# A decoder kernel's opening: a third buffer for early weight pieces, a fixed order on VectorE, C earlier, x loaded by chunk

## The chip, the cores and the metric

The kernel runs on one core of a Trainium2 chip. The metric is the device time of one execution in microseconds (us); less is better. The core's engines work side by side, each through its own queue in order: TensorE (PE) for matmuls, VectorE (DVE), ScalarE (ACT), GpSimd (POOL), and SyncE (SP), which issues most of the DMAs. Times in the trace count from the span's start.

## The reference, cut to what matters

x is (1, 256, 2048) in float32. There are two layers, each a mixer and a SwiGLU feed-forward, with RMSNorm ahead of both.

```python
# layer 0: S5, a diagonal complex state space, 128 groups of 16 channels and 64 states
bu = einsum('blgc,gpc->blgp', norm(x), bb)            # complex
s[k] = lb * s[k-1] + bu[k]                            # scan over the 256 tokens
y = einsum(s_re, c_re) - einsum(s_im, c_im) + d_skip * norm(x)
g = gelu(y); gl = g @ w_glu                           # 2048 x 4096
h = x + gl[..., :2048] * sigmoid(gl[..., 2048:])
h = h + swiglu(norm(h))                               # 2048 -> 5632 -> 2048
# layer 1: sliding-window attention, 32 heads, then the same feed-forward, then a last RMSNorm
```

## The kernel before, in words

Everything is float32. A large matrix product takes each operand as two parts, high and low, and adds three products (`products`, L763). The weights come in 332 pieces of 512 x 512. Each piece is loaded by SP (L107, 1 MB, two raw buffers), then split: ACT copies the high half (L121), DVE subtracts it from the piece for the low half (L122). `Weights.place` says where the two halves go, a tile of 16 KB per partition: three places in rotation, two from the pool `wq` and one from `wp`. `wp` is opened only after the S5 stage has closed its pool, so pieces 0 to 5 have two places. `Weights.next` gives the next piece, and splits up to two further ones and loads up to four further ones ahead. For each piece PE does 24 matmuls (L765 to L767) against 512 columns.

The S5 stage (`s5`) works on 64 pairs of groups, in two halves of 32 pairs and four quarters `t`. Tokens are cut into 64 chunks of four, so that a state steps once per chunk. First x is normed into `xs` (`scaled`, L398, by half). `products(t)` makes the input tables X[t] with POOL (L419) and DVE (L424, L427), ACT copying one part. `tokens(t)` turns xs into U on PE (L436). `states(t, b)` turns X on PE (L448), multiplies with U (L459), and ACT copies the sums into V of the half (L461). Then `step(hf)` (L497, L500, L502) is one step of that half's scan on DVE, three operations; each half has 62 of them, each dependent on the last.

Beside that: `pc` and `dd` (L506, L508) turn the skip weights `d_skip` from `drows`, which POOL fills (L267). POOL makes Cq (L560 to L562), PE and ACT turn it into Cg and C1 (L571, L577). POOL makes the tables T from Cg (`first_states`). `kernels(hf)` makes the tables M on PE (L613 to L625) for the tokens of the same chunk (`own_tokens`, L647). `copied` (L656) brings the scan's states from V to St, and `outputs` (L669) multiplies St with T. `end(qs, ...)` does the outputs of two quarters `q`, GELU (L676), and turns the result into gt, high half on ACT (L690), low half on DVE (L691). (0, 2) are the quarters of the first half, (1, 3) of the second.

Four weight pieces of GLU's first chunk (`EARLY = 4`) are used inside S5, on gt of the first half, while the second scan still runs. Pieces 4 to 7 follow on gt of the second half (`glu`, c == 0), then the other chunks of GLU, with two accumulations `pa` and `pb` for 512 columns each. At the end of a chunk, h gets the product (L880 to L882). x is loaded into h, two DMAs of 1 MB (L1108). Steps put in `left` run between the pieces of a later product.

The order of instructions on each engine is not the program's. A planner simulates the engines: of the instructions that it takes as ready, it puts the one that stands first in the program. `pin` (`keep_in_program_order`) ties an instruction behind the one traced just before it on its engine, and does nothing else: instructions traced after a pinned one can still be put ahead of it. A tile of a tag has that tag's count of buffers, and a new tile waits for the release of an older one.

Of the kernel before, what the change touches and what calls it, by code (L numbers as in the profile page):

```python
# [9 lines left out]
F32 = mybir.dt.float32  # L10
# [7 lines left out]
P = 128  # L18
# [10 lines left out]
NS = 64  # L29
GC = 16  # L30
EARLY = 4
L = 4
NK = T // L
PAIRS = G // 2
# [12 lines left out]
def bc(ap, axis, n):  # L47

    v = ap.unsqueeze(axis)
    shape = list(v.shape)  # L50
    shape[axis] = n
    return v.to_broadcast(shape)
# [3 lines left out]
def kernel(  # L56
# [22 lines left out]
    def bank(shape, name="ps"):  # L79
        return ps.tile(shape, F32, tag="ps", name=nm(name))  # L80
# [9 lines left out]
    class Weights:  # L90
        def __init__(self):
            self.src, self.raw, self.hl = [], [], []
            self.early = {}
            self.used = 0
            self.limit = 0

# [12 lines left out]

        def place(self, i):  # L110

            pool, n = (wp, 1) if i % 3 == 0 and i > 3 else (wq, 2)
            return pool.tile([P, 2, 4, 512], F32R, tag="w", name=nm("w"), bufs=n)

        def split(self, upto, keep=lambda ins: ins):
# [69 lines left out]
    def s5(early_piece):  # L185
# [3 lines left out]
        with st:  # L189
# [3 lines left out]
            def big(shape, name):  # L193
                return sp.tile(shape, F32, tag="b8", name=nm(name), bufs=5)
# [5 lines left out]
                return slice(g2 * NS, (g2 + 1) * NS)  # L200


            Vt = [sp.tile([P, NK, 2, 32], F32, name=f"V{hf}") for hf in range(2)]

            U = sp.tile([P, 4, 16, NK], F32, name="U")

# [57 lines left out]

            drows = sp.tile([PAIRS, 2, L, GC], F32, name="drows")
            PL.memset(drows, 0.0)
            PL.tensor_copy(drows[:, :, 3], drow.rearrange("a (g c) -> a g c", g=2))  # L267


            gb = [bank([P, 512], "gb") for _ in range(2)]  # L270
# [145 lines left out]
            def products(t):  # L416
                tmp = big([P, 3, 2, 16, GC], "tmp")
                for j in (2, 1, 0):
                    PL.tensor_tensor(tmp[:, j], bc(LIs[:, 2 - j].rearrange("p (h f) -> p h f", h=2)  # L419
                                                   [:, :, 16 * t : 16 * t + 16], 3, GC),  # L420
                                     of_groups(B2, t), op=ALU.mult)
                for j in (2, 1, 0):
                    pa = bank([P, 2, 16, GC], "pa")
                    V.tensor_tensor(pa, bc(LR[:, 2 - j].rearrange("p (h f) -> p h f", h=2)  # L424
                                           [:, :, 16 * t : 16 * t + 16], 3, GC),
                                    of_groups(B1, t), op=ALU.mult)
                    V.tensor_tensor(X[t][:, :, :, j].rearrange("p a g c -> p (a g) c"),  # L427
                                    pa.rearrange("p h f c -> p (h f) c"),
                                    tmp[:, j].rearrange("p h f c -> p (h f) c"), op=ALU.add)
                S.copy(X[t][:, :, :, 3].rearrange("p (h a) g c -> p h (a g) c", h=2), of_groups(B1, t))  # L430

            def tokens(t):
                for b in range(2):
                    pu = bank([P, 4, 2, NK], "pu")
                    for i in range(4):
                        PE.transpose(  # L436
                            pu[:, i].rearrange("p h k -> p (h k)"),
                            xs[:, t // 2, 8 * (t % 2) + 4 * b + i].rearrange("p g j c -> p (g j c)"), ident,
                        )
                    S.copy(  # L440
                        U[:, t].rearrange("p (h a) k -> p h a k", h=2)[:, :, 4 * b : 4 * b + 4],
                        pu.rearrange("p a h k -> p h a k"),
                    )
# [21 lines left out]
            def states(t, b):  # L465
                ahead.append((t, b, turned_x(t, b)))
                if len(ahead) > 1:
                    flush()

            def flush():  # L470
                t, b, xt = ahead.pop(0)
                added(t, b, xt)
# [5 lines left out]
            def scan_tables(hf):  # L478
                scan.append(bank([P, 2, 2, 2, 32], "scan"))
                re, im = (LPT[:, 3, ri].rearrange("p (h f a) -> p f h a", h=2, f=2)[:, hf] for ri in range(2))  # L480
                for o, v, f in ((0, re, 1.0), (1, re, 1.0), (2, im, 1.0), (3, im, -1.0)):
                    S.mul(scan[hf][:, 0, o // 2, o % 2].rearrange("p (h a) -> p h a", h=2), v, f)
# [1 line left out]

            reached = [1, 1]

            def step(hf, parts=1):

                reached[hf] += 1
                k = reached[hf]  # L490
                n = 32 // parts
                ws, pr = scan[hf][:, 0], scan[hf][:, 1]
                vs = []
                for i in range(parts):
                    part = slice(n * i, n * (i + 1))
                    t_ = pr[..., part]
                    V.tensor_tensor(t_, ws[..., part], bc(Vt[hf][:, k - 1, :, part], 1, 2), op=ALU.mult)  # L497
                    vs.append((Vt[hf][:, k, :, part], t_))
                for v, t_ in vs:
                    V.tensor_tensor(v, v, t_[:, 0], op=ALU.add)  # L500
                for v, t_ in vs:
                    V.tensor_tensor(v, v, t_[:, 1, ::-1], op=ALU.add)  # L502


            pc = bank([P, PAIRS], "pc")
            PE.transpose(pc, drows.rearrange("a g j c -> a (g j c)"), ident[:PAIRS, :PAIRS])  # L506
            dd = lp.tile([P, PAIRS, GC], F32, name="dd")
            V.tensor_tensor(dd, bc(pc, 2, GC), bc(idm, 1, PAIRS), op=ALU.mult)  # L508
            products(0)
            tokens(0)  # L510
            products(1)
# [4 lines left out]
                states(0, b)  # L516
            scan_tables(0)
            products(2)
            products(3)
            for b in range(4):  # L520
                states(1, b)
# [15 lines left out]
            V.tensor_tensor(u, u, w, op=ALU.subtract)  # L537
            V.tensor_tensor(q_[:, 1], u, iv, op=ALU.mult)

            step(0)  # L540
            step(0)
            tokens(2)
            step(0)
            for b in range(4):
                states(2, b)
                step(0)
                step(0)
            tokens(3)
            scan_tables(1)
            for b in range(4):  # L550
                states(3, b)
                step(0)
                step(0)
            flush()


            Cq = big([G, GC, 2, NS], "Cq")
            c2 = big([G, GC, 2, NS], "c2")
# [7 lines left out]
            for ri in range(2):  # L566
                for e in range(2):
                    pt = bank([P, 8, PAIRS], "pc")
                    for c in range(8):
                        for g2 in range(2):  # L570
                            PE.matmul(pt[rows(g2), c], Cq[:, 8 * e + c, ri], ident[:, g2::2], start=True, stop=True)  # L571
                    S.mul(Cg[:, ri, :, 8 * e : 8 * e + 8], pt.rearrange("p c a -> p a c"), 1.0 - 2 * ri)
            C1 = big([P, G, GC], "C1")
            for i in range(GC // 4):
                pt = bank([P, 4, G], "pc")
# [141 lines left out]
            while reached[0] < NK - 1:  # L717
                step(0)
                if reached[0] + 1 in cuts:
                    k1 = reached[0] + 1  # L720
                    for q in (0, 2):
                        pin(copied(q, cuts[cuts.index(k1) - 1], k1))
                if reached[0] < NK - 1:
                    step(1)

            W.split(1, pin)
            for i in range(4):
                step(1)

            def early():  # L730
                early_piece(gt, 0, 0)
                for q in (1, 3):
                    St[q] = big([P, 2, 16, NK], "St")
                    pin(copied(q, 0, 32))
                for half, q in ((0, 2), (1, 0), (1, 2)):
                    early_piece(gt, half, q)

            end((0, 2), early, lambda: None, pin)
            while reached[1] < NK - 1:
                step(1)  # L740
            for q in (1, 3):
                own_tokens(q)
                pin(copied(q, 32, NK))
            end((1, 3), lambda: None, lambda: W.split(EARLY + 1, pin))
        return gt

    def rms_scale(pool, ssq, shape, keep=lambda ins: ins, between=lambda: None):
# [116 lines left out]
        return wp.tile([P, 512], F32, tag=name, name=nm(name), bufs=bufs)  # L864

    def glu(norm):
        for c in range(NCH):
            if c == 0:
                pa, pb = accs
                for _, half, q in G_ORDER[EARLY:8]:  # L870
                    piece(accs[half], gt[q], q == 0, q == 3)
                while left:
                    left.pop(0)()
            else:
                pa = linear(gt)
                pb = linear(gt)
            for t in range(2):
                hc = h[t][:, 512 * c : 512 * c + 512]
                sg = tmp2("act")
                S.activation(sg, pb[t], AF.Sigmoid)  # L880
                V.tensor_tensor(sg, pa[t], sg, op=ALU.mult)
                V.tensor_tensor(hc, hc, sg, op=ALU.add)  # L882
                norm.chunk(c, t)
# [219 lines left out]
    wp = ctx.enter_context(tc.tile_pool(name="wp", bufs=1))  # L1103
    h = [wp.tile([P, D], F32, name=f"h{t}") for t in range(2)]

    def load_h():
        for t in range(2):
            nc.sync.dma_start(h[t], x[t * P : (t + 1) * P, :])  # L1108

    left.append(load_h)  # L1110

    n0 = Norm(0)
    glu(n0)
    n1 = Norm(1)
# [32 lines left out]
```

## Time and profile before

| | |
|---|---|
| time, median of 3 runs | 2056.07 us (2054.76 to 2057.02) |
| time of the profiled execution | 2056.38 us |
| its span | 2054.6 us |
| PE busy | 1995.3 us (97%), 10692 matmuls |
| DVE busy | 1090.7 us (53%) |
| ACT busy | 859.1 us (42%) |
| POOL busy | 86.2 us (4%) |
| weights' high halves (L121), low halves (L122) | 332 of 1.916 us, 332 of 2.295 us |
| HBM read | 356.90 MB, 175 GB/s over the span |

The profiled execution's time is 1.8 us longer than its span. The page cuts the span into 40 slices of 51 us and gives each engine's busy share in tenths: PE has 6, 8, 7, 8 in the first four slices and 9 in nearly all the others. The line PEclk has 8, 9, 8, 9 there and 9 after (9 is 90% or more). So what isn't PE's own work lies almost wholly in the first 200 us, the S5 stage and GLU's beginning.

### The profile page before, as it was taken

The page shows a single profiled execution, that of the slowest core. Times are in us where ns is not written, and L with a number is a line of the kernel's source. Part 1 is how long each engine was busy: PE and PEld are TensorE (multiplying, and loading weights), DVE is VectorE, ACT ScalarE, POOL GpSimd, SP SyncE. Part 2 cuts the span into 40 slices and gives each one's busy share as a digit, 9 for nine tenths or more (in the row PEclk, how much of TensorE's full clock was granted, in tenths as well). Part 3 has the DMA queues.
Part 4 walks back from the last instruction along what each step waited for, and adds up shares of the span by engine and source line. Part 5 has one row for each costly group of instructions (what it writes and reads, how often), then busy time and mean ns, then how long its engine had stood idle before and what let it go on. Part 6 is the DMA issues. An engine that isn't in the chain of part 4 may idle for free.

```text
span 2054.6 us, 25198 instructions
## 1 busy us (share of the span) xinstructions
PE 1995.3 (97%) x10692; PEld 1648.8 (80%) x10692; DVE 1090.7 (53%) x1347; ACT 859.1 (42%) x867; POOL 86.2 (4%) x66
## 2 busy tenths in 40 slices
PE   6878999999999999999999999999999999999998
PEld 5766888888888888888887777888888888888886
DVE  6955445444544454454466775544454445444545
ACT  5544445334334433433455445443333343343333
POOL 5630000000000000000000000000000000000000
PEclk8989999999999999999999999999999999999999
DMA  5026566555556555555555434565566555555564
GB/s 126 2 83 216 185 187 197 190 186 192 195 186 191 190 192 191 190 193 186 183 186 173 130 102 160 174 196 187 185 195 194 186 194 194 186 192 195 184 194 154
DMA packets 182514, 360.62 MB, mean 176 GB/s; under 512 B 10369, under 2 KB 10433, under 8 KB 182017
## 3 DMA queue, kind: packets, MB, share of 16 engines
q1 hardware_dynamic: 181392, 355.56, 53.7%
q8 instruction: 83, 1.36, 0.3%
q10 hardware_dynamic: 578, 2.14, 0.3%
q0 software_dynamic: 432, 1.33, 0.2%
q14 instruction: 29, 0.24, 0.0%
HBM read 356.90 MB, written 2.10 MB: 175 GB/s over the span
## 4 chain that ended last, share of the span: by engine, by line
PE 92%; DVE 4%; ACT 1%; issue 1%; DMA 1%; POOL 0%; SPq 0%; DVEq 0%; ACTq 0%; POOLq 0%
PE acc L767 29%; PE acc L765 29%; PE acc L766 29%; DVE scan L497 1%; PE tr L894 1%; PE pv L459 1%; DVE w L122 1%; DVE V L502 1%; DVE V L500 1%; ACT w L121 1%; PE tr L805 1%; PE po L1041 0%; PE tr L1030 0%; POOL tmp L419 0%; PE px L448 0%
## 5 line engine op out<-in xcount | busy, mean ns | idle before, releaser
L122 DVE TENSOR_TENSOR w<-raw,w 128x2048 fp32r<-128x2048 f32 x332 | 761.8, 2295 | 856.2 <-ACT w L121 856.2
L121 ACT ACTIVATE w<-raw 128x2048 fp32r<-128x2048 f32 x332 | 636.0, 1916 | 968.4 <-PE acc L767 845.8
L765 PE MATMUL acc<-w,xT 128*128 128x512 f32 x1568 | 613.6, 391 | 0.0
L767 PE MATMUL acc<-w,xT 128*128 128x512 f32 x1568 | 612.1, 390 | 0.0
L766 PE MATMUL acc<-w,xT 128*128 128x512 f32 x1568 | 611.5, 390 | 0.0
L767 PEld LDWEIGHTS acc<-w,xT 128*128 128x128 f32 x1568 | 294.5, 188 | 61.9 <-issue 1.0
L765 PEld LDWEIGHTS acc<-w,xT 128*128 128x128 f32 x1568 | 294.6, 188 | 61.1 <-issue 1.3
L766 PEld LDWEIGHTS acc<-w,xT 128*128 128x128 f32 x1568 | 294.7, 188 | 60.5 <-issue 0.5
L765 PE MATMUL acc<-w,hT 128*128 128x512 f32 x704 | 275.6, 391 | 0.0
L766 PE MATMUL acc<-w,hT 128*128 128x512 f32 x704 | 273.9, 390 | 0.0
L767 PE MATMUL acc<-w,hT 128*128 128x512 f32 x704 | 273.8, 390 | 0.0
L765 PEld LDWEIGHTS acc<-w,hT 128*128 128x128 f32 x704 | 132.3, 188 | 27.9 <-ACT hT L896 1.2
L767 PEld LDWEIGHTS acc<-w,hT 128*128 128x128 f32 x704 | 132.2, 188 | 27.6
L766 PEld LDWEIGHTS acc<-w,hT 128*128 128x128 f32 x704 | 132.3, 188 | 27.0
L767 PE MATMUL acc<-w,gt 128*128 128x512 f32 x256 | 102.2, 400 | 4.4 <-DVE gt L691 4.4
L765 PE MATMUL acc<-w,gt 128*128 128x512 f32 x256 | 102.2, 399 | 3.7 <-ACT w L121 3.7
L766 PE MATMUL acc<-w,gt 128*128 128x512 f32 x256 | 102.1, 399 | 1.9 <-DVE w L122 1.9
L767 PEld LDWEIGHTS acc<-w,gt 128*128 128x128 f32 x256 | 49.4, 193 | 15.7 <-DVE gt L691 5.3
L765 PEld LDWEIGHTS acc<-w,gt 128*128 128x128 f32 x256 | 49.4, 193 | 14.5 <-ACT w L121 4.1
L766 PEld LDWEIGHTS acc<-w,gt 128*128 128x128 f32 x256 | 49.5, 193 | 12.3 <-DVE w L122 2.2
L921 DVE TENSOR_TENSOR h<-h,acc 128x512 f32<-128x512 f32 x64 | 43.5, 687 | 24.7 <-PE acc L767 24.7
L907 ACT ACTIVATE act<-acc,ry 128x512 f32<-128x512 f32 x44 | 30.2, 690 | 59.8 <-PE acc L767 59.8
(240 smaller groups left out, 1225.0 us busy)
## 6 DMA issues: line engine op xcount, KB each, us to landing
raw<-in_ffn_w_gate_dram SPq DMA_DIRECT2D x88, 1024.0 KB, 5.2
raw<-in_ffn_w_up_dram SPq DMA_DIRECT2D x88, 1024.0 KB, 5.2
raw<-in_ffn_w_down_dram SPq DMA_DIRECT2D x88, 1024.0 KB, 5.1
raw<-in_s_w_glu_dram SPq DMA_DIRECT2D x32, 1024.0 KB, 5.2
raw<-in_attn_w_qkv_dram SPq DMA_DIRECT2D x20, 1024.0 KB, 5.1
raw<-in_attn_w_o_dram SPq DMA_DIRECT2D x16, 1024.0 KB, 5.1
xk<-in_x_dram SPq DMA_DIRECT2D x8, 256.0 KB, 7.9
h<-in_x_dram SPq DMA_DIRECT2D x2, 1024.0 KB, 10.4
```

Source lines behind the costliest of these rows:

```text
L121: keep(S.activation(hi, self.raw[i], AF.Copy))
L122: keep(V.tensor_tensor(lo, self.raw[i], hi.bitcast(F32), op=ALU.subtract))
L459: PE.matmul(pv[r, ri, i], xt[r, i, ri], U[r, t, 4 * b + i], start=True, stop=True)
L497: V.tensor_tensor(t_, ws[..., part], bc(Vt[hf][:, k - 1, :, part], 1, 2), op=ALU.mult)
L500: V.tensor_tensor(v, v, t_[:, 0], op=ALU.add)
L502: V.tensor_tensor(v, v, t_[:, 1, ::-1], op=ALU.add)
L765: PE.matmul(acc, x_[:, 0], w[0][:, a], start=first, stop=False)
L766: PE.matmul(acc, x_[:, 0], w[1][:, a], start=False, stop=False)
L767: PE.matmul(acc, x_[:, 1], w[0][:, a], start=False, stop=last)
L805: PE.transpose(pt[:, t], h[t][:, kt * P : (kt + 1) * P], ident)
L907: S.activation(s, pg[t], AF.Silu, scale=r[0][:, t : t + 1])
L921: V.tensor_tensor(hc, hc, acc[t], op=ALU.add)
```

## The change

- **A third place.** V of the two halves get tags of their own. `W.third` takes a tile with the first half's tag, V0, and so gets that buffer once the first half's states have been copied out. Pieces 1 and 4 go there; of the others, one in three goes to `wp` (7, 10, ...), the rest to `wq`.
- **Skip rows.** The copy into `drows` moves from POOL to ACT; pc and dd move from ahead of products(0) to behind products(2).
- **C earlier.** Cq, c2 and Cg move from behind the last states to between states(2) and tokens(3). C1 stays behind the last states. The first scan's steps are spread otherwise in the program.
- **VectorE's order.** After the first half's scan ten steps of the second scan stand in the program instead of four; then come gt's low halves, piece 1's split and one pinned step (its multiplication), four more steps, and the rest behind the early pieces. In the loop a step of the second scan is taken only while it is more than `LEAD = 20` steps behind the first scan.
- **Pieces 4 and 5.** Piece 4 is split ahead of the second half's own tokens, piece 5 where 4 was split before.
- **x by chunk.** h is loaded 512 columns at a time, ahead of each of GLU's four chunks, pinned on SP.

```diff
         def place(self, i):
-            pool, n = (wp, 1) if i % 3 == 0 and i > 3 else (wq, 2)
+            if i in (1, 4):
+                return self.third()
+            pool, n = (wp, 1) if i % 3 == 1 else (wq, 2)
...
-            Vt = [sp.tile([P, NK, 2, 32], F32, name=f"V{hf}") for hf in range(2)]
+            Vt = [sp.tile([P, NK, 2, 32], F32, tag=f"V{hf}", name=f"V{hf}") for hf in range(2)]
+            W.third = lambda: sp.tile([P, 2, 4, 512], F32R, tag="V0", name=nm("w3"))
...
-            PL.tensor_copy(drows[:, :, 3], drow.rearrange("a (g c) -> a g c", g=2))
+            S.copy(drows[:, :, 3], drow.rearrange("a (g c) -> a g c", g=2))
...
-            pc = bank([P, PAIRS], "pc")            # and pc's transpose and dd, L505 to L508
             products(0)
...
             products(2)
+            pc = bank([P, PAIRS], "pc")            # the same lines
             products(3)
...
-            step(0)
-            step(0)
+            lead(2)
             tokens(2)
-            step(0)
+            lead(1)
             for b in range(4):
                 states(2, b)
-                step(0)
-                step(0)
-            tokens(3)
-            scan_tables(1)
-            for b in range(4):
-                states(3, b)
-                step(0)
-                step(0)
-            flush()
+                lead(2)
             # Cq, c2 and Cg, L557 to L572
+            lead(4)
+            tokens(3)
+            scan_tables(1)
+            for b in range(4):
+                states(3, b)
+                lead(2)
+            flush()
             # C1, L573 to L578
...
-                if reached[0] < NK - 1:
+                if reached[1] + LEAD < reached[0] < NK - 1:
                     step(1)
             W.split(1, pin)
-            for i in range(4):
+            for i in range(10):
                 step(1)
             def early():
+                W.split(2, pin)
+                step(1, keep=pin)
+                for i in range(4):
+                    step(1)
                 early_piece(gt, 0, 0)
...
             while reached[1] < NK - 1:
                 step(1)
+            W.split(EARLY + 1)
             for q in (1, 3):
                 own_tokens(q)
                 pin(copied(q, 32, NK))
-            end((1, 3), lambda: None, lambda: W.split(EARLY + 1, pin))
+            end((1, 3), lambda: None, lambda: W.split(EARLY + 2, pin))
...
+        def load_h(c):
+            for t in range(2):
+                cs = slice(512 * c, 512 * c + 512)
+                tc.keep_in_program_order(nc.sync.dma_start(h[t][:, cs], x[t * P : (t + 1) * P, cs]))
         for c in range(NCH):
+            left.append(partial(load_h, c))
...
-    def load_h():
-        for t in range(2):
-            nc.sync.dma_start(h[t], x[t * P : (t + 1) * P, :])
-    left.append(load_h)
```

## Rows read from the trace of the kernel before

**Rows 1.** Waits of PE, 0 to 200 us: engine line <- releaser: total, times, longest.
```profile
PE py L669 <- ACT St L656: 13.4, 1, 13.4
PE pc L506 <- POOL drows L267: 7.5, 1, 7.5
...
PE acc L767 <- DVE gt L691: 4.4, 2, 3.9
PE acc L765 <- ACT w L121: 3.7, 1, 3.7
...
PE py L669 <- issue: 2.7, 2, 1.5
...
PE acc L766 <- DVE w L122: 1.9, 1, 1.9
```

**Rows 2.** Windows: stretch, its length, busy time of each engine, clock, DMA.
```profile
200.00:220.00 20.00, 20.00 (x90) 16.54 (x90) 8.24 (x7) 7.60 (x4) 0.00 (x0) 1.00 0.60 187
```

**Rows 3.** DVE in order of time, 20 to 66 us: start, length, [idle before, releaser].
```profile
22.38 4.04 DVE L398 SCALAR_TENSOR_TENSOR xs<-xk,r,gb 128x512 f32<-128x512 f32 x6
28.62 1.23 DVE L508 TENSOR_TENSOR dd<-pc,idm 128x1024 f32<-128x1024 f32 x1 [2.20 <-PE pc L506]
29.76 1.29 DVE L424 TENSOR_TENSOR pa<-LR,B 128x512 f32<-128x512 f32 x2
...
50.53 0.30 DVE L497 TENSOR_TENSOR scan<-scan,V 128x128 f32<-128x128 f32 x1 [4.25 <-ACT V L461]
...
65.71 0.50 DVE L497 TENSOR_TENSOR scan<-scan,V 128x128 f32<-128x128 f32 x2 [1.70 <-ACT V L461]
```

**Rows 4.** PE in order of time, 64 to 116 us.
```profile
64.98 3.96 PE L571 MATMUL pc<-ident,Cq 128*64 128x64 f32 x128
...
109.05 6.18 PE L669 MATMUL py<-T,St 64*64 64x64 f32 x256 [13.40 <-ACT St L656]
```

**Rows 5.** DVE in order of time, 108 to 136 us.
```profile
108.27 0.29 DVE L497 TENSOR_TENSOR scan<-scan,V 128x128 f32<-128x128 f32 x1
...
111.19 3.25 DVE L122 TENSOR_TENSOR w<-raw,w 128x2048 fp32r<-128x2048 f32 x1 [0.69 <-ACT w L121]
...
121.24 2.48 DVE L691 TENSOR_TENSOR gt<-pt,gt 128x512 fp32r<-128x512 f32 x4
...
131.66 2.29 DVE L122 TENSOR_TENSOR w<-raw,w 128x2048 fp32r<-128x2048 f32 x1 [3.47 <-ACT w L121]
...
135.30 0.22 DVE L502 TENSOR_TENSOR V<-V,scan 128x64 f32<-128x64 f32 x1
```

**Rows 6.** PE in order of time, 121 to 155 us.
```profile
121.98 0.79 PE L767 MATMUL acc<-w,gt 128*128 128x512 f32 x1 [3.94 <-DVE gt L691]
...
145.93 2.10 PE L647 MATMUL py<-M,U 64*64 64x64 f32 x128
...
153.67 1.32 PE L669 MATMUL py<-T,St 64*64 64x64 f32 x73 [1.25 <-issue]
```

**Rows 7.** Chain that ended last, in order of time, one matmul after gt.
```profile
123.19 0.43 PE acc L767
```

**Rows 8.** ACT in order of time, 116 to 190 us.
```profile
116.41 2.09 ACT L690 CAST gt<-pt 128x512 fp32r<-128x512 f32 x4
...
137.28 4.04 ACT L656 COPY St<-V 128x1024 f32<-128x1024 f32 x2
...
152.73 3.74 ACT L121 ACTIVATE w<-raw 128x2048 fp32r<-128x2048 f32 x2
...
171.37 0.63 ACT L1065 ACTIVATE bias<-bias 128x512 f32<-128x512 f32 x1 [11.86 <-issue]
...
189.38 1.28 ACT L880 ACTIVATE act<-acc 128x512 f32<-128x512 f32 x2 [0.70 <-PE acc L767]
```

**Rows 9.** DMA issues: tile, queue, count, KB each, median us to landing.
```profile
raw<-in_s_w_glu_dram SPq DMA_DIRECT2D x32, 1024.0 KB, 5.2
...
h<-in_x_dram SPq DMA_DIRECT2D x2, 1024.0 KB, 10.4
```

More of the change, by code (lines that the diff above doesn't have):

```diff
@@ L31 @@
 EARLY = 4
+LEAD = 20
 L = 4
@@ L93, in __init__ @@
             self.early = {}
+            self.third = None
             self.used = 0
@@ L485, in s5, with step @@
             reached = [1, 1]
-            def step(hf, parts=1):
+            def step(hf, parts=1, keep=lambda ins: ins):
                 reached[hf] += 1
@@ L496, in step @@
                     t_ = pr[..., part]
-                    V.tensor_tensor(t_, ws[..., part], bc(Vt[hf][:, k - 1, :, part], 1, 2), op=ALU.mult)
+                    keep(V.tensor_tensor(t_, ws[..., part], bc(Vt[hf][:, k - 1, :, part], 1, 2), op=ALU.mult))
                     vs.append((Vt[hf][:, k, :, part], t_))
@@ L502, in step @@
                     V.tensor_tensor(v, v, t_[:, 1, ::-1], op=ALU.add)
-            pc = bank([P, PAIRS], "pc")
-            PE.transpose(pc, drows.rearrange("a g j c -> a (g j c)"), ident[:PAIRS, :PAIRS])
-            dd = lp.tile([P, PAIRS, GC], F32, name="dd")
-            V.tensor_tensor(dd, bc(pc, 2, GC), bc(idm, 1, PAIRS), op=ALU.mult)
             products(0)
@@ L518, in s5 @@
             products(2)
+            pc = bank([P, PAIRS], "pc")
+            PE.transpose(pc, drows.rearrange("a g j c -> a (g j c)"), ident[:PAIRS, :PAIRS])
+            dd = lp.tile([P, PAIRS, GC], F32, name="dd")
+            V.tensor_tensor(dd, bc(pc, 2, GC), bc(idm, 1, PAIRS), op=ALU.mult)
             products(3)
@@ L538, in s5, with lead @@
             V.tensor_tensor(q_[:, 1], u, iv, op=ALU.mult)
-            step(0)
-            step(0)
+            def lead(n):
+                for i in range(n):
+                    step(0)
+            lead(2)
             tokens(2)
-            step(0)
+            lead(1)
             for b in range(4):
                 states(2, b)
-                step(0)
-                step(0)
-            tokens(3)
-            scan_tables(1)
-            for b in range(4):
-                states(3, b)
-                step(0)
-                step(0)
-            flush()
+                lead(2)
             Cq = big([G, GC, 2, NS], "Cq")
```

## The prediction, made before the result was known

> **What bounds the kernel now.** I read the waits of TensorE (PE) first, then VectorE's (DVE's) and ScalarE's (ACT's) order of time, and last the windows. From about 190 us to the end PE is full: 20.00 of 20.00 us with 90 matmuls at clock 1.00 [rows 2], 0.222 us for one, and nothing of the diff takes a matmul from there. The bound of the rest is the opening, 190 us long, and there PE's waits stand in one list [rows 1]: 13.4 us for the states' copy, 7.5 for the skip rows of POOL, 4.4 for gt, 3.7 and 1.9 for weight pieces. Idle time is not gain by itself; each wait has to be followed to what sets its end.
>
> The skeleton of the opening is two scans of 62 steps on DVE, a chain for each half of the pairs. The first starts at 50.53 [rows 3] and runs alone, 16 steps in 13.5 us (0.843 each), until 64.0. DVE then idles 1.70 us for the second half's V; from 65.71 to 108.27 [rows 3, 5] it runs 46 pairs of steps, one of each scan, 0.925 a pair. So a step of the second scan costs 0.08 beside the first scan and 0.843 alone. At 108.27 the first scan is over, its states are copied, and PE goes from 109.05 on [rows 4].
>
> **The change, part by part.** All times are of the profiled execution, 2056.38 us (span 2054.6), 0.3 over the median of the runs, 2056.07.
>
> *Skip rows and dd.* DVE has six parts of xs done at 26.42, idles 2.20 for PE's transpose pc, which waits for POOL's drows, spends 1.23 on dd, and only then begins products(0) at 29.76 [rows 3]. PE's token transposes queue behind the same pc. Afterwards the copy is on ACT, and pc and dd stand behind products(2). At least 2.20 + 1.23 = 3.4 goes. With the first four xs done at 22.38 + 4 x 0.67 = 25.1, products(0) can start 4.7 earlier. If its three multiplications, which need no xs, fill earlier idle time, 3 x 0.65 = 2.0 more goes, 6.7. I take 4.7, the nearest to the rows, as the four xs stand ahead of products(0) in the program. dd's 1.23 then hides in the 4.25 that DVE idles before the first step [rows 3]; without that cover it costs 1.23. The copy's price on ACT is the third rival. First scan: 45.8.
>
> *C ahead of the second half's last V.* Making C there puts 128 small matmuls, 3.96 us [rows 4], before states(3), so the second scan can start at 65.71 - 4.7 + 4.0 = 65.0. Alone until then, the first scan does 19.2 / 0.843 = 22.8 steps, and the other 39.2 in pairs take 36.3: end 101.3. If the planner sets the second scan too early again and the 1.70 idle stays, it is 103.1. I take 102.3, a gain of 6.0. In this frame the new LEAD holds nothing back: the program's lead is 23 steps at the loop, above 20. The products of POOL that follow C start earlier; nothing waits for them [rows 1].
>
> *VectorE's order.* Before, 49 steps of the second scan, piece 0's low half (3.25) and 8 further steps ran ahead of gt's low halves, which began at 121.24, 13.0 after the first scan's end [rows 5], with the high halves ready from about 117 [rows 8]. The pinned step now lets exactly 48 steps go ahead: (102.3 - 65.0) / 0.925 = 40.3 are done in pairs, 7.7 x 0.843 = 6.5 follow, with piece 0 9.7. gt's high half comes 8.7 after the scan, so DVE still decides, by 1.0. PE goes on 0.74 after the low half's begin, as at 121.98 [rows 6]: 102.3 + 9.7 + 0.7 = 112.7, 9.3 earlier. Queued behind the pinned step are the last 14 steps, and through them the states of the second half.
>
> *Pieces 0 to 3.* These ran from 121.98 to 145.93 [rows 6]; the first 13 matmuls went out every 0.43 us [rows 7], 1.2 GHz, after PE had stood 4 us, and cost 2.7 more than at 0.222. With a gap of about 1 us I drop that: 21.3 us, to 134.0; with it 136.7. The third place itself removes no wait here, as PE showed none between these pieces; it is what allows piece 4 ahead of the outputs.
>
> *Second scan and outputs.* From 112.0 DVE does gt (2.48), 14 steps (11.8) and four low halves (4 x 2.29 = 9.2): end 135.5, against 135.52 before [rows 5]. A late piece with steps queued behind it, as the one of 3.47 [rows 5], would add up to 3.5. Two copies of 4.04 together [rows 8] bring the first states at about 137.8, the second at 139.8, while PE is through pieces and own tokens at 136. The outputs took 148.0 to 154.99 [rows 6], 2.7 of it stalls called issue [rows 1]. With all stalls they end at 144.9, with none at 142; I take 144.0, since a wait ahead of them may give the sequencer time. Gain so far 11.0.
>
> *Pieces 4 and 5 split earlier.* ACT put both, 3.74, between the two activations of the outputs [rows 8]; one stays, so the high halves come 1.9 earlier, and with one low half less DVE follows: 2.0 with the small wait for gt after 158.
>
> *Pieces 6 and 7.* PE waited 3.7 + 1.9 = 5.6 [rows 1] for piece 6, then did some 14 matmuls at 0.43, 2.8 more. ACT stood 11.86 until 171.37 at the attention bias (L1065), with piece 6 behind it [rows 8]. Now piece 6 has a place of wq and its raw buffer is free when piece 4 is split, some 25 us earlier; I expect it ahead of the bias. 8.4 goes; half of it if only one of the two pieces gets ahead.
>
> *x by chunk.* Two DMAs of 1 MB become eight of 256 KB. Each is pinned behind the DMA traced before it on SP; for chunk 0 that is raw piece 11, which waits for piece 9's split, about 23 us after the outputs' end. Landing takes between the raw pieces' 5.2 and h's 10.4 [rows 9]; the sums at piece 7's end (189.38 before [rows 8], 34.4 after the outputs' end, now 24) would wait 4 to 9 us, and behind them DVE's splits and PE's first transposes of h. PE has two pieces, 48 matmuls or 10.7 us, ready; only the transposes, after the first of these (29.4), can stop it: by nothing if the planner lets the second go first, by 5.3 if x takes the 10.4 and the sums 1.3 more. I take 1.3, nearer to the first, as the planner plans with a landing too. The six later DMAs have 40 us each.
> The Trainium skill ("DMA: Bandwidth & Descriptors", Queues, rings and completion order) says that each DMA engine takes descriptors of one ring in order, so chunk 0 would stand behind the whole megabyte of piece 11. By that rule, and an estimate of 5.2 plus half of 5.2 from the raw pieces' row, the stop is 2.7 and the time 2037.7; h's 10.4, twice a raw piece's beside weight loads, agrees as far as it goes.
>
> Sum: 11.0 + 2.0 + 8.4 - 1.3 = 20.1; 2056.38 - 20.1 = 2036.3.
>
> **The rivals.**
> *A: the bias still leads ACT.* For it: the planner did that once, for a transfer it took as landed. Against: piece 6 is ready far earlier. The bias lands 16.4 after the outputs' end [rows 6, 8], now perhaps 15.3; with the bias' own 0.6 and piece 6's 1.9 and 2.3 it is split 20.1 after, and PE, with pieces 4 and 5 from 2.5 on, wants it at 13.2: 6.9 wait and 2.8 clock, 2046.0.
> *B: the second scan starves, slower.* Place: PE's queue. If states(3) goes behind C1 and the kernels, the block from 64.98 to 95.65 [rows 4], 30.7 us, the second scan starts 26.7 later than forecast. Each us of that turns 1.08 paired steps into lone ones: 0.91 later, less 0.09 for a quicker first scan, 0.82. 26.7 x 0.82 = 21.9: 2058.2. It decides from a start at about 89.5. Against: the program has states(3) first, and C waits for nothing late.
> *C: the skip rows hold ACT.* If their copy is queued ahead of x's squares, ACT stands until they land, 28.6 at the latest, when dd ran on them [rows 3]. The xs move from 22.38 by up to 6.2 and the 4.7 is gone: 2047.2 at most. Against: POOL took them behind all its first products, so they were planned late.
> *D: the change doesn't do what it says.* The planner again lifts other work ahead of gt's low half and PE keeps waiting; the second scan's copies end as late as before. Then only the small wait for gt, some 2 to 3 us, goes: 2053.5. Against: the pinned step carries all later ones behind it.
>
> **How the numbers follow.** Forecast 0.66, A 0.13, C 0.06, D 0.07, B 0.05, other losses 0.03. The likeliest case has its own ends: best 2.0 (multiplications early), 1.0 (no idle), 2.0 (no stalls), 1.3 (x in time) make 2030.0; worst 1.3 (only 3.4 early), 0.8 (idle stays), 3.5 (a late piece), 0.9 (all stalls) and 4.0 (x late) make 2046.8. With A and C the range is 2029.5 to 2048.0. What this kernel's measurement can tell from no change is about 0.2%, 4.1 us. Faster by more 0.86, within 0.06 (most of D), slower 0.08.
>
> **What would show it.** The first step of the scan near 45.8; the second scan near 65 without idle before it; the first scan's end near 102; PE on gt from 112.7 at full clock; the outputs of the second half at 138 to 144, behind a wait for the St copy in place of pieces; no ACT idle at L1065 with a piece behind it; piece 7's end near 169. The prediction is wrong if DVE stands for a weight piece in the second scan, if the bias or the skip rows hold ACT, or if PE stops for chunk 0 of x by more than 3 us.

## The result, and the profile after

The changed kernel takes 2042.86 us (median of 4 runs, 2042.44 to 2042.92) against 2055.53 for the kernel before in the same comparison (4 runs, 2054.76 to 2057.02): ratio 0.9937, 95% interval 0.992 to 0.9954, so 12.7 us faster. The forecast was 2036.3 with a range of 2029.5 to 2048.0: sign and range hold, the likeliest value is 6.6 too low. The profiled execution took 2042.92 with a span of 2041.1, 13.5 shorter than the span before.

The sum of the page: PE does the same 10692 matmuls in 7.5 us less busy time (1995.3 before), and its idle time falls by 6.0. So part of the gain is clock: between 110 and 135 us the granted clock rose from 0.78 to 0.99 of full speed.
```profile
PE 1987.8 (97%) x10692; PEld 1643.5 (81%) x10692; DVE 1093.0 (54%) x1347; ACT 859.5 (42%) x868; POOL 84.4 (4%) x65
```
PE's waits of the first 200 us, changed kernel (waiter <- releaser: total, times, longest):
```profile
PE py L676 <- ACT St L663: 17.1, 2, 16.1
PE pu L442 <- DVE xs L404: 6.9, 1, 6.9
...
PE tr L817 <- DVE h L900: 3.2, 1, 3.2
...
PE pt L690 <- ACT y L683: 1.6, 1, 1.6
```
Against [rows 1] the 7.5 us for the skip rows have become 6.9 for xs, the 4.4 for gt and the 3.7 and 1.9 for piece 6 are gone, and 3.2 for h (`tr L817 <- DVE h L900`) is new. The states' copy is the longest wait still, and longer than before: this list does not say what a wait is worth, which is why the stages follow.

DVE in order of time, changed kernel (start, length, what, [idle before, releaser]); it answers to [rows 3, 5].
```profile
24.45 4.04 DVE L404 SCALAR_TENSOR_TENSOR xs<-xk,r,gb 128x512 f32<-128x512 f32 x6
...
37.22 1.23 DVE L524 TENSOR_TENSOR dd<-pc,idm 128x1024 f32<-128x1024 f32 x1 [0.42 <-PE pc L522]
...
47.05 0.30 DVE L503 TENSOR_TENSOR scan<-scan,V 128x128 f32<-128x128 f32 x1 [4.21 <-ACT V L467]
...
66.12 0.30 DVE L503 TENSOR_TENSOR scan<-scan,V 128x128 f32<-128x128 f32 x1 [1.07 <-ACT V L467]
...
103.97 0.30 DVE L503 TENSOR_TENSOR scan<-scan,V 128x128 f32<-128x128 f32 x1
...
113.07 2.48 DVE L698 TENSOR_TENSOR gt<-pt,gt 128x512 fp32r<-128x512 f32 x4
...
137.39 0.22 DVE L508 TENSOR_TENSOR V<-V,scan 128x64 f32<-128x64 f32 x1
```
First step 47.05 (50.53 before), first scan's end 103.97 (108.27), gt's low halves 113.07 (121.24), second scan's end 137.61 (135.52).

PE in order of time, changed kernel, from gt to the first transposes of h; the first row answers to [rows 6], as do the outputs.
```profile
113.81 0.51 PE L779 MATMUL acc<-w,gt 128*128 128x512 f32 x1
...
135.12 1.96 PE L654 MATMUL py<-M,U 64*64 64x64 f32 x90
137.66 1.15 PE L654 MATMUL py<-M,U 64*64 64x64 f32 x38 [0.58 <-DVE V L508]
139.76 2.95 PE L676 MATMUL py<-T,St 64*64 64x64 f32 x184 [0.95 <-ACT St L663]
143.71 1.28 PE L676 MATMUL py<-T,St 64*64 64x64 f32 x72 [0.99 <-issue]
...
148.43 0.47 PE L777 MATMUL acc<-w,gt 128*128 128x512 f32 x1
...
171.30 0.50 PE L778 MATMUL acc<-w,gt 128*128 128x512 f32 x1 [0.58 <-DVE w L126]
...
181.44 1.72 PE L817 MATMUL tr<-ident,h 128*128 128x128 f32 x8 [3.24 <-DVE h L900]
182.81 0.78 PE L777 MATMUL acc<-w,gt 128*128 128x512 f32 x1
183.39 0.63 PE L778 MATMUL acc<-w,gt 128*128 128x512 f32 x1
```
PE is on gt 8.2 earlier and at the full clock, through pieces 0 to 3 10.8 earlier (135.12 against 145.93), and through the outputs 10.0 earlier (144.99 against 154.99). From 148.43 to 171 there is no stop. Then comes what the kernel before did not have: 3.24 us for h, and behind it matmuls 0.43 apart, the half clock (1.2 of 2.4 GHz), as in [rows 7].

ACT in order of time, changed kernel, answers to [rows 8]:
```profile
142.97 3.74 ACT L125 ACTIVATE w<-raw 128x2048 fp32r<-128x2048 f32 x2
146.57 1.23 ACT L683 ACTIVATE y<-py 128x256 f32<-128x256 f32 x4
147.62 2.12 ACT L697 CAST gt<-pt 128x512 fp32r<-128x512 f32 x4
155.25 1.92 ACT L125 ACTIVATE w<-raw 128x2048 fp32r<-128x2048 f32 x1 [5.50 <-PE acc L779]
166.48 0.63 ACT L1083 ACTIVATE bias<-bias 128x512 f32<-128x512 f32 x1 [9.32 <-DMA bias<-in_attn_b_qkv_dram]
167.02 3.70 ACT L125 ACTIVATE w<-raw 128x2048 fp32r<-128x2048 f32 x2
...
172.03 1.09 ACT L898 ACTIVATE act<-acc 128x512 f32<-128x512 f32 x2
```
Two rows speak against the forecast. Two pieces, 3.74, still stand between the outputs' activations. And the scaling of the attention bias still leads ACT: it now idles 9.32 us before L1083, with pieces 8 and 9 (3.70) and GLU's sigmoid behind it.

### The profile page after: what moved, and what is told of

Its sections match the earlier page's. It is cut to its first block, busy times and chain, and to the rows that moved or that the text cites. A ratio compares the mean times of both kernels' runs of the same rounds, so it can differ in the third digit from the quotient of the medians.

```text
span 2041.1 us, 25206 instructions
## 1 busy us (share of the span) xinstructions
PE 1987.8 (97%) x10692; PEld 1643.5 (81%) x10692; DVE 1093.0 (54%) x1347; ACT 859.5 (42%) x868; POOL 84.4 (4%) x65
## 4 chain that ended last, share of the span: by engine, by line
PE 91%; DVE 5%; ACT 2%; DMA 2%; issue 1%; POOL 0%; SPq 0%; DVEq 0%; ACTq 0%; POOLq 0%
PE acc L777 28%; PE acc L779 28%; PE acc L778 28%; PE tr L912 1%; DVE scan L503 1%; DVE w L126 1%; PE pv L465 1%; ACT w L125 1%; DVE V L508 1%; DVE V L506 1%; PE tr L817 1%; DMA raw<-in_s_w_glu_dram 1%; PE po L1059 0%; PE tr L1048 0%; DMA bias<-in_attn_b_qkv_dram 0%
## 5 line engine op out<-in xcount | busy, mean ns | idle before, releaser
L778 PE MATMUL acc<-w,gt 128*128 128x512 f32 x256 | 100.3, 392 | 0.6 <-DVE w L126 0.6
L777 PE MATMUL acc<-w,gt 128*128 128x512 f32 x256 | 100.7, 393 | 0.0
L779 PE MATMUL acc<-w,gt 128*128 128x512 f32 x256 | 99.8, 392 | 0.0
```

The costliest lines, as they stand in the source:

```text
L777: PE.matmul(acc, x_[:, 0], w[0][:, a], start=first, stop=False)
L778: PE.matmul(acc, x_[:, 0], w[1][:, a], start=False, stop=False)
L779: PE.matmul(acc, x_[:, 1], w[0][:, a], start=False, stop=last)
```

## The experiments

All but e10 are the changed kernel with one or two edits. Runs of four comparisons (the result, e1 to e4, e5 to e8, e9 to e12) are set beside each other by their ratio to the kernel before; spans are those of the profiled executions. A span is one execution: in versions that leave the opening as it is, the scan's first step stands anywhere from 46.49 us (e2) to 47.30 (e1, e12), so a difference of spans under about 1 us shows nothing by itself.

| | time, us | ratio to before, 95% | span |
|---|---|---|---|
| before / after | 2055.53 / 2042.86 | 0.9937 (0.992, 0.9954) | 2054.6 / 2041.1 |
| e1 x whole | 2041.8 | 0.9935 (0.9923, 0.9948) | 2040.4 |
| e2 bias pinned late | 2035.42 | 0.9903 (0.989, 0.9917) | 2033.7 |
| e3 piece 6 behind gt | 2041.09 | 0.993 (0.9918, 0.9943) | 2039.0 |
| e4 skip rows back | 2045.92 | 0.9955 (0.9941, 0.9968) | 2044.9 |
| e5 no third place | 2043.1 | 0.9947 (0.9934, 0.9959) | 2043.1 |
| e6 DVE's order back | 2045.8 | 0.9958 (0.9945, 0.997) | 2045.5 |
| e7 C back | 2045.6 | 0.9953 (0.994, 0.9967) | 2045.1 |
| e8 xs first | 2043.16 | 0.9941 (0.9928, 0.9953) | 2039.9 |
| e9 e2 + e3 | 2034.44 | 0.9899 (0.9885, 0.9912) | 2032.6 |
| e10 before, bias pinned late | 2046.57 | 0.9957 (0.9945, 0.997) | 2044.7 |
| e11 e2 + x whole | 2036.57 | 0.9909 (0.9895, 0.9922) | 2034.8 |
| e12 e2, no third place | 2035.84 | 0.9905 (0.989, 0.992) | 2034.0 |

**Which of two causes makes PE stop at 178: x by chunk, or the bias.** e1 loads x in two DMAs of 1 MB, as before.
```diff
-            left.append(partial(load_h, c))
+    left.append(load_h)          # once, ahead of glu; h[t] <- x rows, 1 MB each
```


> x in two DMAs of 1 MB again, free of order, so that they go ahead of raw pieces 8 to 11; all else as changed. If chunk 0's late landing makes PE's stop at the first transposes of h (3.24 us, then 8 transposes and 6 matmuls at half clock, together some 5), it goes: 2037.5 to 2038.5. If the rival is right that the megabytes of x only push raw pieces 8 and 9 back and PE stops for them instead: 2042 to 2045.

The wait for h went, and the time stayed. PE in order of time, e1, every row of 165 to 180 us with idle time before it:
```profile
171.99 0.50 PE L777 MATMUL acc<-w,gt 128*128 128x512 f32 x1 [1.79 <-ACT w L125]
174.32 0.50 PE L778 MATMUL acc<-w,gt 128*128 128x512 f32 x1 [1.82 <-DVE w L126]
```
ACT stood 12.63 us at the bias until 169.51, so piece 8 itself was late: 3.6 us of PE's time for the 3.2 that went. The bias' transfer took 8.2 us in place of 5.5, beside the two megabytes. The expectation that x by chunk was the cause has failed, and the rival's reason with it: pieces 8 and 9 are split right behind the bias without idle time, so their own loads were there. As e1 moves the bias too, it needs e2 beside it.

e2 keeps x by chunk and fixes the place of the bias' scaling in ACT's queue.
```diff
-                S.mul(b, b, HD ** -0.5)
+                tc.keep_in_program_order(S.mul(b, b, HD ** -0.5))
```


> The attention bias' multiplication on ACT (L1083) pinned behind its predecessor in the program, so that pieces 8 and 9 no longer stand behind it. If the 9.3 us that ACT stood there is what makes raw pieces 10 and 11, and x behind 11, late, they come 2.5 to 5.7 us earlier and most of PE's stop of 5 goes: 2038 to 2040. If the bias is harmless, since PE waited only 0.6 for a piece: 2042.5 to 2043.

2035.42, better than expected. Its windows of PE (stretch, length, busy, clock, DMA share, GB/s), and those of the changed kernel after them:
```profile
150.00:170.00 20.00, 20.00 (x90) 1.00 0.63 201
170.00:200.00 30.00, 30.00 (x138) 1.00 0.70 232
```
```profile
150.00:170.00 20.00, 20.00 (x90) 1.00 0.50 168
170.00:200.00 30.00, 26.18 (x111) 0.94 0.66 213
```
With the bias out of the way PE is full from 150 us on. The DMA share between 150 and 170, 0.63 against 0.50, fits the link: raw buffers come free as pieces are split, so a split behind the bias holds back transfers too. In DVE's order of e2, h's sum waits a mere 0.17 for its chunk, 6.4 us earlier than the 180.70 of the changed kernel:
```profile
174.32 1.31 DVE L900 TENSOR_TENSOR h<-h,act 128x512 f32<-128x512 f32 x2 [0.17 <-DMA h<-in_x_dram]
```
On SP the chunk was issued at 168.85 in place of 173.93, because raw pieces 10 and 11 ahead of it got their buffers earlier.

e10 puts the same line into the kernel before and nothing else.
```diff
-                S.mul(b, b, HD ** -0.5)
+                tc.keep_in_program_order(S.mul(b, b, HD ** -0.5))
```


> The kernel before with one edit: the attention bias' scaling pinned behind the work ahead of it in the program. Own theory: the waits of 3.7 and 1.9 us for piece 6 go, and the half clock behind them (2.8), so 8.4 of 2055.5: 2046.3 to 2048.0, and the largest single term of the forecast is to be had without anything else of the change. Rival: the weight pieces behind it are late by their own loads (ACT waited 6.1 and 1.9 us for raw pieces right after), so PE only stops a piece later and half or less comes: 2050.5 to 2053.5.

2046.57: the own expectation's 2046.3 to 2048.0 holds. PE's windows of e10, which before had 24.40 of 30.00 us busy at clock 0.89 in the last stretch:
```profile
170.00:200.00 30.00, 30.00 (x138) 1.00 0.66 216
```
So one line gives 8.2 us to the kernel before, two thirds of what the whole change gave; on top of it the change gives another 11.2 (2046.57 to 2035.42).

**The two pieces between the activations.** In the changed kernel piece 4 is split ahead of the outputs, but the planner lifted piece 6 into the free place. e3 keeps it behind gt.
```diff
                 pa, pb = accs
+                W.split(EARLY + 3, tc.keep_in_program_order)
```


> Piece 6's split pinned behind gt of the second half. The forecast's 2.0 for one piece less between the two activations did not come, as piece 6 took piece 4's place there. If that is the cause, PE starts piece 4 some 2 to 2.5 us earlier: 2040.4 to 2041. If the transposes or the clock set that start, or x's landing gives it back: 2042.5 to 2043.2.

2041.09, span 2.1 shorter: 0.1 above the expected band, and the intervals of the two ratios overlap. The stretch from the outputs' last matmuls to piece 4, 4.72 us in the changed kernel, is 3.17 (143.05 to 146.22). ACT of e3, one piece between the activations, piece 6 after them:
```profile
141.64 1.93 ACT L125 ACTIVATE w<-raw 128x2048 fp32r<-128x2048 f32 x1
...
147.35 2.00 ACT L125 ACTIVATE w<-raw 128x2048 fp32r<-128x2048 f32 x1
```
e9 joins e2 and e3.

```diff
@@ the lines of e2 and e3
```


> Both mended places of the changed kernel together: the attention bias' scaling pinned behind the work that stands ahead of it in the program, and piece 6 kept behind gt of the outputs. Own theory: the two losses lie at different times (piece 6 at 143 to 150 us, the bias at 157 to 176 us) and add up, so 1.2 to 2.1 us come off the 2035.4 of the pinned bias alone: 2033.3 to 2034.2, with PE on piece 4 near 146.3 and piece 7's end near 166.7. Rival: with the bias out of the way ACT is early enough everywhere and the next limit after piece 7 (h's chunk 0, DVE's split of piece 8) takes the 2 us back: 2035.0 to 2035.8.

2034.44, span 2032.6: 1.1 under e2, just between the two expectations and too little to tell from e2 by the ratios. The trace tells it: PE's outputs and its first matmul of piece 4 in e9,
```profile
142.86 1.28 PE L676 MATMUL py<-T,St 64*64 64x64 f32 x72 [1.56 <-issue]
144.07 2.20 PE L690 MATMUL pt<-ident,y 128*128 128x128 f32 x16
146.02 0.47 PE L777 MATMUL acc<-w,gt 128*128 128x512 f32 x1
```
3.16 us from one to the other, where e2 has 4.71 and the changed kernel 4.72, and the sigmoid at piece 7's end stands at 167.39 against 168.74 in e2. It is the fastest version, 20.4 us under its before.

**The change's parts, undone one at a time.** e4 puts the skip rows on POOL and dd ahead of products(0) again.
```diff
-            S.copy(drows[:, :, 3], ...)
+            PL.tensor_copy(drows[:, :, 3], ...)
@@ pc and dd stand ahead of products(0) again
```


> Skip rows back on POOL, pc and dd back ahead of products(0); all else as changed. If this part gave what the first step of the scan shows (50.53 to 47.05, 3.5 us), and it goes to the end one for one: 2046.0 to 2046.8. With the forecast's 4.7 it would be 2047.6. If a later wait takes it up: 2043 to 2044.

2045.92: 3.7 us by the ratios, 3.8 by the spans, a little under the expectation. The first step is at 52.08, 5.0 later, the second scan's begin (71.17), the first scan's end (108.9) and gt (118.10) by as much, the second scan's end (141.55) by 3.9. Not all of it need be the skip rows': the first step is also 1.55 later than in the kernel before (50.53), where the skip rows are the same. PE stays at the half clock for one more group of the states there (granted 0.50 from 39 to 42 us, 1.00 in the kernel before), and so it does in e10, which opens as the kernel before does (0.64). This part is worth its 4 by the ratios; about 1.4 of that may be this scatter of the opening.

e5 takes the third place away.
```diff
-            if i in (1, 4):
-                return self.third()
-            pool, n = (wp, 1) if i % 3 == 1 else (wq, 2)
+            pool, n = (wp, 1) if i % 3 == 0 and i > 3 else (wq, 2)
```


> The old rule of places: pieces 0 to 5 share the two of wq, piece 6 goes to wp; all else as changed. If the third place is worth little by itself (piece 2 is split when piece 0 is done, as before, and piece 6 can no longer step between the two activations): 2041 to 2045. If it is what let pieces 4 to 6 be ready ahead of the outputs' end, piece 6 stands behind the attention bias again and PE waits some 7 us with a slow clock after it: 2049 to 2052.

2043.1, in the expected band, span 2.0 over the changed kernel. But here too the bias (161.47, after 10.57 idle) leads pieces 7 and 8, and PE waited 4.1 for h and 1.7 for w, so e12 repeats it with the bias pinned.
```diff
@@ e2's line, and the place of e5
```

> The changed kernel with the pinned bias, and without the third place: early weight pieces in two places of wq and one of wp as before. Own theory: the third place lets piece 2 be split early and one more piece stand ready at the outputs, worth the 2.0 us of span that it was worth with the bias still in the way: 2036.4 to 2038.0. Rival: its worth was only in what the bias held back, and without that it is nothing: 2034.9 to 2036.0.

2035.84, span 0.3 over e2: the rival, but its reason is another. PE of e12, its outputs and the first matmul of piece 4:
```profile
144.44 1.28 PE L674 MATMUL py<-T,St 64*64 64x64 f32 x72 [1.30 <-issue]
145.65 2.19 PE L688 MATMUL pt<-ident,y 128*128 128x128 f32 x16
147.60 0.48 PE L775 MATMUL acc<-w,gt 128*128 128x512 f32 x1
```
Without the third place the outputs end 1.8 later than in e2 (145.72 against 143.88), 0.8 of it already at the scan's first step (47.30 against 46.49), but only one piece stands between their activations, and piece 4 begins 0.3 later (147.60 against 147.31). So the third place earns some 1.0 ahead of the outputs, and piece 6 in it spends 1.5 right after. With piece 6 kept out, e9 is 1.4 ahead of e12, and its four runs (2034.27 to 2035.26) all lie below e12's (2035.54 to 2036.15).

e6 gives DVE its old order around the outputs, without the pinned step.
```diff
-            for i in range(10):
+            for i in range(4):
                 step(1)
-                W.split(2, pin)
-                step(1, keep=pin)
-                for i in range(4):
-                    step(1)
```


> Four steps after the first scan again, no piece 1 and no pinned step behind gt; the loop's condition and all else as changed. If the order is worth what the trace shows at gt (low halves 9.1 after the first scan's end for 13.0, and no slow clock), PE restarts about 4 later, does 13 matmuls at half clock, and the outputs come 5 to 6 later: 2047 to 2050. If the second scan's end alone sets the outputs, the order gives nothing, since the steps then run earlier: 2041 to 2044.

2045.8, between the two. gt's low halves of e6 against 113.07 of the changed kernel:
```profile
116.70 2.48 DVE L698 TENSOR_TENSOR gt<-pt,gt 128x512 fp32r<-128x512 f32 x4
```
3.6 later, PE waits 4.2 for gt again, and the outputs end at 149.37, 4.4 later, which is also what the spans differ by. The new order, ten steps, piece 1 and the pinned step together, is worth some 4 us; which of the three does it was not run.

e7 puts C behind the second half's states.

```diff
@@ lead(4), tokens(3), scan_tables(1), the four states(3, b) with lead(2) and flush()
@@ stand ahead of Cq's block again, as before
```


> Cq, c2 and Cg behind the last states again, steps spread otherwise as changed. By the rates of the steps, the second scan then starts some 4 earlier, 4 more of its steps run beside the first scan at 0.08 in place of 0.843, and gt's low half and the second scan's end come 2 to 3 earlier: the early C was a loss, 2039.5 to 2041.5. If the planner again leaves DVE idle for the second half's V, or POOL's tables become late: 2043 to 2046.

2045.6, against the own expectation. The second scan did start earlier, at 62.37, but then 46 steps in pairs instead of 40 held the first scan until 104.9, and the fixed order turned this round. DVE of e7:
```profile
107.84 3.25 DVE L126 TENSOR_TENSOR w<-raw,w 128x2048 fp32r<-128x2048 f32 x1 [1.27 <-ACT w L125]
113.62 2.48 DVE L698 TENSOR_TENSOR gt<-pt,gt 128x512 fp32r<-128x512 f32 x4 [2.52 <-ACT gt L697]
116.91 3.17 DVE L126 TENSOR_TENSOR w<-raw,w 128x2048 fp32r<-128x2048 f32 x1 [0.80 <-ACT w L125]
```
With 46 of the 48 steps done early, DVE reaches gt before the high half is there and idles 2.52, with 14 steps of the scan queued behind it; the second scan's end comes 1.6 later and the outputs' end 1.9. So in this reading C ahead of states(3) doesn't gain by itself, it keeps the first scan alone for longer and lets DVE meet gt's high half without idling. Whether another count for the pinned step would serve the old place of C as well was not tried.

e8 pins products(0)'s first multiplication behind the four xs, to see whether these cost the missing 1.2 us of the first step.

```diff
-            products(0)
+            products(0, pin)     # pins the first pa<-LR,B of the group, xs stand ahead
```


> The first multiplication of products(0) pinned behind the four xs, the order that the forecast took for granted. The planner had put three multiplications and three sums into the chain that makes the norm's r0 and so moved xs from 22.38 to 24.45. If that is why the first step came at 47.05 and not at 45.8, it now comes at 45.5 to 46.2: 2041.4 to 2042.2. If PE's states are bound by X and not by xs: 2042.8 to 2044.

2043.16: no gain, though xs now begin at 21.98. The first step stood at 47.37. The states need X (products) and U (from xs) alike, and the third group of them is 5.1 ahead of the kernel before here and 5.3 in the changed kernel, so the order of the two on DVE doesn't matter. What is missing goes later, at pc and dd (next section).

## Why the prediction was nearly right, and where it failed

| step of the forecast | forecast | after |
|---|---|---|
| first step of the first scan | 45.8 | 47.05 |
| second scan begins | 65.0 | 66.12 |
| first scan's end | 102.3 | 103.97 |
| PE on gt | 112.7, full clock | 113.81, full clock |
| pieces 0 to 3 end | 134.0 | 135.12 |
| second scan's end | 135.5 | 137.61 |
| outputs' end | 144.0 (-11.0) | 144.99 (-10.0) |
| pieces 4 and 5 earlier | -2.0 | +0.2 (piece 4 at 148.43 for 158.20) |
| pieces 6 and 7 without stops | -8.4 | about -9.7, 0.5 of it the small wait for gt |
| lost again at x's chunk 0 | +1.3 | +6.0 |
| sum, profiled | -20.1 | -13.5 |

*The skeleton held.* Every mark up to the outputs is 1.0 to 2.1 us late and in the forecast's order. The first 1.25 come from the first step, and there a term of the sum failed: "dd's 1.23 then hides in the 4.25 that DVE idles before the first step". The planner put six instructions of products(0) ahead of xs, which begin at 24.45 instead of 22.38 [rows 3]; that cost nothing, since PE's third group of states (pv) stands at 35.83 for 41.13 before, 5.3 earlier and more than the 4.7 of the forecast. Then pc and dd come, and PE stops twice. The fourth and fifth group of the changed kernel, and the fifth of the kernel before:
```profile
38.59 1.15 PE L465 MATMUL pv<-U,xt 64*64 64x64 f32 x32 [0.82 <-DVE dd L524]
...
40.98 1.15 PE L465 MATMUL pv<-U,xt 64*64 64x64 f32 x32 [0.66 <-ACT xt L456]
```
```profile
44.46 1.15 PE L459 MATMUL pv<-U,xt 64*64 64x64 f32 x32
```
So 1.8 of the 5.3 are gone, and the 3.5 left are the first step's gain. The forecast had priced dd without cover at 1.23. e8 loses 2.0 at the same place. That dd is the cause is read from the waits, no run moved it alone. The second scan's end lost another 1.0, three short idles of DVE (0.65, 0.82, 0.20) for high halves, less than the 3.5 allowed. The skip rows' copy on ACT took 0.22 us at 21.66 after 0.55 of idle: rival C had no part in it. Rival B is out too: states(3) did go first.

*Pieces 4 and 5.* The step "one stays" between the activations failed. One left and piece 6 came into its place; e3 and e9 show that some 1.6 us were there (4.72 to 3.17, 4.71 to 3.16).

*Pieces 6 and 7, and x.* The forecast asked of the bias only whether it would hold up piece 6. It didn't: piece 6 went ahead, and PE was full from 148.43 to 171. Piece 7's end came to about 169.9 (worked out: in e2 the sigmoid after it starts at 168.74, and there piece 4 began 1.12 earlier), 19.5 before the 189.38 of [rows 8]. But only 13.5 reach the end of the span; 6.0 are lost between 170 and 186: waits of 0.58 and 3.24, transposes of 1.72 where e2 takes 1.03, and six matmuls at 0.43 instead of 0.227, 1.2; together 5.7. The forecast gave this place 1.3 and laid it to x. e1 shows that x whole leaves it as large, e2 that it is the bias. So rival A's mechanism was right and its piece wrong: the bias held pieces 8 and 9, where the rival had it hold piece 6 at 9.7. Pinning it takes 7.4 us off the span (2041.1 to 2033.7); 1.1 of these are there before the bias, as piece 4 begins at 147.31 in e2 and at 148.43 in the changed kernel, so 6.3 are the bias'.

By the prediction's own last sentence its mechanism was wrong here: the bias held ACT (9.32), and PE stopped for chunk 0 by more than 3 us (3.24). The time still fell into the range, as its worst case had 4.0 more for a late x and rival A 2046.0. That a loss of about that size came at x's place from another cause is luck.

How the bias makes PE stop can be followed in four steps: ACT stands at L1083 until 166.48; pieces 8 and 9 are split 167 to 171; only then do raw pieces 10 and 11 go out on SP, and x's chunk 0 behind them at 173.93; its sum, behind piece 10's low half on DVE (178.50 to 180.7), is done too late for the transposes. Chunk 0's landing (about 6.7 us from its issue) and that low half end within 0.2 us of each other, and DVE has no idle time between the low half and the sum; so either alone would have kept the sum back as long, and with the bias pinned neither is late.

Why the bias comes so late can be read on POOL, which issues its transfer. POOL in order of time, kernel before, then changed kernel:
```profile
159.02 0.23 POOL L938 IOTA ji<- 128x128 int32 x1 [37.82 <-ACT gt L690]
```
```profile
155.67 0.23 POOL L956 IOTA ji<- 128x128 int32 x1 [48.43 <-PE acc L779]
...
159.80 0.54 POOL L971 DMA_DIRECT2D bias<-in_attn_b_qkv_dram  x1
```
The outputs end 10.0 earlier, but POOL's first instruction behind S5 comes only 3.4 earlier, as it now waits for a matmul on gt and not for gt's cast. It does so in every version with the third place, and in none without. In e5, which only takes the third place away, the bias is scaled 15.6 after the outputs' end, in the changed kernel 21.5 after; rival A had reckoned with 15.3. The third place is a tile of S5's memory that piece 4 still reads, which would explain it. So the change itself kept the bias back, by some 5 us (166.48 against 161.47 in e5). What an earlier bias is worth by itself was not run.

The sentence on the Trainium skill ("DMA: Bandwidth & Descriptors", Queues, rings and completion order) agrees with the trace as far as it goes: the chunks of 256 KB landed in 5.6 us, raw pieces of four times the size in 5.3, as if most of the chunks' landing were spent behind the pieces ahead; no run shows the order itself. It would have made 2037.7, not 2042.9. x by chunk is worth little either way: e11 loads x whole with the bias pinned.
```diff
@@ the lines of e1 and e2
```


> The changed kernel with the pinned bias, and x loaded whole again, two DMAs of 1 MB, instead of by chunk. Own theory: with the bias out of the way neither way of loading stops PE; h's chunk 0 was in time by 0.2 us of DVE's wait with chunks, and whole it is far earlier: within 0.7 us of 2035.4, 2034.7 to 2036.1. Rival: the 2 MB go ahead of raw pieces 10 and 11 and make these late for their splits, as h and the raw pieces share the DMA engines: 2037 to 2039, with PE waiting for w around piece 10.

2036.57, span 1.1 over e2, 0.7 of it at the scan's first step (47.23 against 46.49), and 0.5 of PE's waits at h; 0.5 above the expected band, under what the measurement tells apart. The first half of the rival is seen, as ACT waits 7.61 us for piece 9's raw data where e2 waits 2.76, but PE doesn't stop for w.

With the bias pinned the change gives 20.9 of span, against a forecast of 20.1 that hung on the bias being harmless; 8.2 are had by the pinned line alone (e10).

## What to carry to other kernels

When a wait is forecast to go because its victim moves ahead, ask what stands behind the same blocker next: a small instruction that waits for its own transfer at the head of an in-order queue costs whoever is queued there, here pieces 8 and 9 in place of piece 6. Mend the blocker first, as one line did for 8.2 us, and then measure the larger change on top, since in its shadow other parts look worth more or less than they are (the third place: 2.0 of span with the bias in the way, 0.3 without, 1.4 once piece 6 is kept out too, each with up to 0.8 of the opening's scatter in it). A place made free in a queue was filled by the planner with the next ready work, so a gain from "one less" needs the next one kept out too. And memory that is kept in use for longer holds back whatever gets it next, here the issue of the bias.

## What the runs showed of the hardware

The clock can fall after PE has gone on again. In the changed kernel the matmuls after the stop of 3.24 were 0.43 apart from the second on; e1 has two stops of 1.79 and 1.82 with one matmul between them, then runs three matmuls about 0.23 apart, and only then goes to the half clock, for eight matmuls. PE of e1 in order of time:
```profile
175.11 0.49 PE L778 MATMUL acc<-w,gt 128*128 128x512 f32 x1
175.40 0.63 PE L779 MATMUL acc<-w,gt 128*128 128x512 f32 x1
175.83 0.63 PE L777 MATMUL acc<-w,gt 128*128 128x512 f32 x1
```
Its window of 170 to 180 us was granted 0.83 of full speed on the mean. After single stops of 0.58 and 1.57 us (changed kernel, 171.30 and 147.58) the matmuls stayed at 0.23 to 0.24. So here two stops that lie close together were paid for like a longer one.

DVE took 2.29 us for the low half of a weight piece by itself. Beside POOL's products it took longer, by nearly what was left of POOL's instruction when it began: 2.76 with 0.61 left (changed kernel, 106.63, POOL until 107.24), 3.25 with 1.10 left and 3.17 with 1.02 left (e7, 107.84 and 116.91, POOL until 108.94 and 117.93). It went the other way round too: the product that POOL began 1.07 after the DVE instruction of 107.84 took 4.41 in place of 2.34.
```profile
108.91 4.41 POOL L604 TENSOR_TENSOR T<-T,tmpT 128x1024 f32<-128x1024 f32 x1
```
In these cases each engine looks to have waited for the other's instruction to end, though times on POOL are rough.
